# A two-layer encoder in fp32 parts: pairs that are split at once and pairs that stay whole take turns one by one in both MLPs

## The chip, the cores and the metric

The kernel runs on one core of a Trainium2 chip. Its engines are TensorE (PE: matrix products, with weight loads shown as PEld), VectorE (DVE), ScalarE (ACT), GpSimd (POOL) and SyncE (SP, which issues DMAs). Each works through its own queue in order, and semaphores between the queues carry the dependences. The metric is the device time of one execution in microseconds.

## The reference: what is computed

The input is 512 tokens of 1024 numbers. Layer 0 is a hybrid attention (grouped-query and latent heads), layer 1 a neighbourhood attention on an 8 x 64 grid, and behind each stands an MLP; a norm ends it. Only the MLPs matter here:

```
def sq_relu_mlp(h, w_up, w_down):
    u = jax.nn.relu(h @ w_up)
    return (u * u) @ w_down

h = h + sq_relu_mlp(rmsnorm(h, norm_ffn[layer]), ffn_w_up[layer], ffn_w_down[layer])
```

`w_up` is 1024 x 4096 and `w_down` 4096 x 1024, all in float32.

## The kernel before

**Numbers in two parts.** To keep float32 accuracy, every operand of a product is held as a high part (rounded to the matmul's format, `F32R`) and a low part (what the rounding left). Each product is three matmuls: high by high, high by low, low by high. So every weight chunk and every activation must be split: ScalarE copies the high part, VectorE subtracts it from the source to get the low part.

**Products with seven parts.** A part of the MLP's products is done by a scheme of the class `Seven`: a 2 x 2 arrangement of blocks is multiplied with seven block products in place of eight, at the price of sums of weights before (GpSimd, L357 to L359) and sums of results behind (VectorE, L459 to L462, after a copy of ScalarE at L458). A weight chunk of this kind is `seven_chunk`: SP loads 256 rows by 256 columns (L352) into a raw tile; GpSimd makes the sums; ScalarE makes the high part `whi` (L363, three buffers), VectorE the low part `wlo` (L364, four buffers). One call of `Seven.run`, a **pass** below, gives two result tiles of 128 x 512 (a **pair**): four chunks, each with 7 x 3 = 21 matmuls (L450 to L452), so 84 matmuls. Passes take turns between two groups of PSUM banks (named s, t, t, o and mm, mm, mm, s), so that the results of one are taken away during the next.

**The stages of one MLP.** `first_product` makes the tiles of the squared relu. Its first stage makes six of them, and a part of the second product follows. Its second stage, the long first product, has 13 passes, numbered 0 to 12 here, for the remaining 26 tiles. Then come `product8`, which uses eight of these tiles as plain split operands, a product by `Seven` over pairs that `convert` turns into its operands, and a rest. The first MLP's long first product runs from 322 to 451 us of the profile and the second's from 883 to 1013 us.

**Two kinds of pairs.** In a pass, the end `evac` receives the pair in one tile `w_` of 128 x 1024. For kind 0, **split at once** (`pair_evac`, L1400), the pair is one of the four whose eight tiles `product8` needs: two more tiles are taken for its parts. For kind 1, **whole** (`raw_evac`, L1395), `w_` is kept as it is for later stages. Either way `finish` (L1380) does the rest in three steps, which the loop in `stage` puts behind the 15th, 22nd and 25th of the 28 block products of the next pass: Relu (L1382) and Square (L1383) on ScalarE; for a split pair, then, for each of its two tiles a copy on ScalarE (L1388) and a subtraction on VectorE (L1389). These four kinds of instructions are held in the order of the program (`held`); most others are placed by the planner of the framework, which orders each engine's queue by its own cost model and by what is ready.

**Memory.** Tiles of 128 x 1024 come from 32 slots (`Slot`), given out in turn, the longest free first. The long first product's operand takes 14 of them. Each whole pair keeps one; the first two split pairs keep two each and give `w_` back, the third keeps one and the fourth none, since three of their tiles lie in spare buffers. Weight chunks load into a free slot if more than three are free, else into one of four raw buffers; they are asked for five chunks ahead (`LOAD`) and split two ahead (`AHEAD`).

The order of the kinds is a list in `stage`, L1450 and L1451, which is called with `n` = 8 tiles to be split and 16 or 14 that stay whole for the seven-part product, and 2 or 4 more for the rest. The list of split pairs' row numbers also gives `product8` the rows of `w_down`, and that of whole pairs gives them to the next product.

Of the kernel before, what the change touches and what calls it, by code (L numbers as in the profile page):

```python
# [35 lines left out]
def encoder_kernel(ctx: ExitStack, tc: tile.TileContext, ins, out, dbg=None):  # L36
# [1304 lines left out]
    def first_product(l):  # L1341
# [68 lines left out]
        def plain():  # L1410
            four = product(w, 0, xp, tiles(0, 512), ev, lambda n: [mmb(), mmb(), mmb(), sbk()])
            two = product(w, 0, xp, tiles(512, 256), ev, lambda n: [sbk(), ob()], kstep=4)
            for n, _ in enumerate(four):
                if n == (11 if l == 0 else 13):
                    norm()
                if n == 14:
                    x_sums(0)
                    x_sums(1)
            for n, _ in enumerate(two):
                if n == 4:  # L1420
                    x_sums(2)
                if n == 6:
                    x_sums(3)
            flip[0] = 1
            for s_ in X:
                s_.free()
            state["plain"] = True
# [9 lines left out]
        def ahead():  # L1437
            state["ids"] = x7.plan(w, P * state["c"])

        def stage(n, raw=0, more=0):  # L1440


            at = [], []
            if not state["plain"]:
                plain()
                at[0].extend(range(0, n, 2))
            nu, nr = (n - len(U)) // 2, raw // 2
            state["n"], state["halves"] = n, raw

            kinds = ([1, 0, 0] * ((nu + 1) // 2))[: nu + (nu + 1) // 2] if nr else [0] * nu  # L1450
            kinds += [1] * (nr + nu - len(kinds)) + [1] * (more // 2)  # L1451
            for i, kind in enumerate(kinds):
                ids = state["ids"]
                if i < nu + nr:
                    at[kind].append(state["c"])
                state["c"] += 2
                if i < len(kinds) - 1:
                    ahead()
                for u, _ in enumerate(x7.run(ids, (pair_evac, raw_evac)[kind])):
                    if u in (14, 21, 24):  # L1460
                        next(state["late"], None)
            if state["c"] == 32:
                x7.free()
            got = U[:n], R[: raw // 2], R[raw // 2 :], at, state["late"]
            U.clear()
            R.clear()
            return got

        return stage, ahead, later


# [603 lines left out]
```

## Time and profile before

| | us |
|---|---|
| median of three runs | 1163.75 (1161.8 to 1165.85) |
| the profiled execution | 1162.95 |
| its span, first to last instruction | 1161.2 |
| TensorE busy | 1146.3 |
| VectorE busy | 901.3 |
| ScalarE busy | 669.2 |
| GpSimd busy | 586.4 |

The rows of the profile name a line of the kernel, an engine, an operation and the tiles written and read (`out<-in`); groups have a count, the busy time, the mean of one in ns and the idle time of the engine before it, with what ended that. Rows in order of time begin with the start and the duration in us and end, where the engine was idle, with the idle time and its releaser in square brackets. A matmul's duration reaches to its modelled end, so successive matmuls overlap: their spacing is read from their starts.

### The profile page before, as it was taken

How to read it: one execution, taken by the hardware profiler on the slowest of the kernel's cores; microseconds unless marked ns; L12 is line 12 of the kernel's file. 1: busy time of each engine (PE TensorE's matmuls, PEld its weight loads, DVE VectorE, ACT ScalarE, POOL GpSimd, SP SyncE). 2: the span in 40 equal slices, each digit the busy share in tenths (PEclk: the TensorE clock that was granted, in tenths of full speed). 3: DMA queues.
4: the chain of work that ended last, by engine and by line, in shares of the span. 5: the costliest groups of instructions: out<-in, count | busy, mean ns of one | idle time of the engine just before them, and what ended most of it. 6: DMA issues, size and time to landing. Idle time of an engine off the chain costs nothing.

```text
span 1161.2 us, 20538 instructions
## 1 busy us (share of the span) xinstructions
PE 1146.3 (99%) x7348; PEld 1022.4 (88%) x7348; DVE 901.3 (78%) x1568; ACT 669.2 (58%) x1135; POOL 586.4 (51%) x719
## 2 busy tenths in 40 slices
PE   9999999999999999999999999999999999999997
PEld 7787888888899999899988998988889999989996
DVE  6887988878868876877785666668996787688865
ACT  6676877755346668543454556555543666774445
POOL 4356252207688992369502232231388799435840
PEclk9999999999999999999999999999999999999999
DMA  7322415222523327723536564433343233381432
GB/s 235 105 77 69 97 55 137 64 69 95 171 77 91 100 83 199 214 88 112 155 92 163 148 175 128 116 110 116 113 143 116 83 92 91 71 202 56 127 119 73
DMA packets 115350, 134.37 MB, mean 116 GB/s; under 512 B 9795, under 2 KB 96752, under 8 KB 115248
## 3 DMA queue, kind: packets, MB, share of 16 engines
q1 hardware_dynamic: 110896, 120.09, 34.9%
q0 software_dynamic: 4032, 12.60, 5.4%
q8 instruction: 58, 0.95, 0.3%
q10 hardware_dynamic: 320, 0.36, 0.1%
q14 instruction: 44, 0.36, 0.1%
HBM read 110.61 MB, written 6.29 MB: 101 GB/s over the span
## 4 chain that ended last, share of the span: by engine, by line
PE 87%; DVE 5%; DMA 2%; issue 2%; ACT 1%; POOL 1%; SPq 0%; DVEq 0%; ACTq 0%; POOLq 0%
PE mm L606 8%; PE mm L607 8%; PE mm L608 8%; PE mm L452 4%; PE mm L450 4%; PE mm L451 4%; PE s L1130 3%; PE o L1118 3%; PE t L450 3%; PE t L452 3%; PE t L451 3%; PE s L608 2%; PE s L606 2%; PE s L607 2%; PE t L1105 2%
## 5 line engine op out<-in xcount | busy, mean ns | idle before, releaser
L606 PE MATMUL mm<-a,whi 128*128 128x512 f32 x428 | 173.8, 407 | 0.2
L364 DVE TENSOR_TENSOR wlo<-a,whi 128x896 fp32r<-128x896 f32 x103 | 130.7, 1272 | 55.3 <-ACT whi L363 54.9
L607 PE MATMUL mm<-a,whi 128*128 128x512 f32 x428 | 169.0, 395 | 0.0
L608 PE MATMUL mm<-a,wlo 128*128 128x512 f32 x428 | 168.9, 396 | 0.0
L363 ACT ACTIVATE whi<-a 128x896 fp32r<-128x896 f32 x103 | 97.6, 948 | 105.0 <-PE o L607 27.6
L233 ACT ACTIVATE whi<-raw 128x1024 fp32r<-128x1024 f32 (+3 forms) x100 | 92.1, 924 | 68.5 <-PE s L607 24.3
L223 DVE TENSOR_TENSOR wlo<-raw,whi 128x1024 fp32r<-128x1024 f32 (+4 forms) x97 | 110.0, 1139 | 27.2 <-ACT whi L233 26.7
L452 PE MATMUL mm<-a,wlo 128*128 128x256 f32 x430 | 120.6, 280 | 0.3 <-DVE wlo L364 0.3
L450 PE MATMUL mm<-a,whi 128*128 128x256 f32 x430 | 120.7, 281 | 0.0
L451 PE MATMUL mm<-a,whi 128*128 128x256 f32 x430 | 120.3, 280 | 0.0
L363 ACT ACTIVATE whi<-raw 128x896 fp32r<-128x896 f32 x61 | 57.9, 952 | 80.5 <-POOL raw L359 37.9
L359 POOL TENSOR_TENSOR a<-a 128x128 f32<-128x128 f32 x103 | 99.3, 964 | 8.1
L364 DVE TENSOR_TENSOR wlo<-raw,whi 128x896 fp32r<-128x896 f32 x61 | 73.2, 1214 | 36.0 <-ACT whi L363 36.0
L358 POOL TENSOR_TENSOR a<-a 128x256 f32<-128x256 f32 x103 | 93.7, 910 | 8.1
L608 PEld LDWEIGHTS mm<-a,wlo 128*128 128x128 f32 x428 | 80.3, 188 | 18.2
L606 PEld LDWEIGHTS mm<-a,whi 128*128 128x128 f32 x428 | 80.5, 188 | 17.2 <-issue 0.8
L607 PEld LDWEIGHTS mm<-a,whi 128*128 128x128 f32 x428 | 80.7, 189 | 15.1 <-DVE a L655 0.3
L1718 POOL TENSOR_SCALAR p<-p,ti 128x256 f32<-128x256 f32 x64 | 36.0, 574 | 105.4 <-DVE ti L1717 90.4
L1138 POOL TENSOR_SCALAR p<-p,ti 128x512 f32<-128x512 f32 x64 | 45.5, 711 | 86.0 <-DVE ti L1137 61.4
L450 PE MATMUL t<-a,whi 128*128 128x256 f32 x312 | 87.7, 281 | 0.0
L452 PE MATMUL t<-a,wlo 128*128 128x256 f32 x312 | 87.3, 280 | 0.0
L451 PE MATMUL t<-a,whi 128*128 128x256 f32 x312 | 87.3, 280 | 0.0
(432 smaller groups left out, 3577.2 us busy)
## 6 DMA issues: line engine op xcount, KB each, us to landing
a<-in_ffn_w_up_dram SPq DMA_DIRECT2D x102, 256.0 KB, 2.8
raw<-in_ffn_w_down_dram SPq DMA_DIRECT2D x34, 512.0 KB, 4.1
raw<-in_ffn_w_down_dram SPq DMA_DIRECT2D x59, 256.0 KB, 2.6
raw<-in_od_w_qkv_dram SPq DMA_DIRECT2D x64, 128.0 KB, 3.0
raw<-in_ffn_w_up_dram SPq DMA_DIRECT2D x12, 512.0 KB, 3.9
wlo<-in_ffn_w_down_dram POOLq DMA_DIRECT2D x12, 512.0 KB, 6.7
a<-a SPq DMA_DIRECT2D x18, 256.0 KB, 3.3
bx<-a SPq DMA_DIRECT2D x32, 128.0 KB, 6.0
```

Of the source, the lines that this page charges most:

```text
L223: z = lambda: (eng or DVE).tensor_tensor(to, src, f32(high), op=ALU.subtract)
L233: ACT.activation(hi[:, 0:m], raw[:, 0:m], AF.Copy)
L358: held(eng.tensor_tensor(r[:, 4:6], r[:, 2:3].to_broadcast([P, 2, P]), r[:, 0:7:6], op=ALU.add))
L359: held(eng.tensor_tensor(r[:, 7], r[:, 3], r[:, 5], op=ALU.subtract))
L363: ACT.activation(hi[:, 0:896], raw[:, 128:1024], AF.Copy)
L364: DVE.tensor_tensor(lo[:, 0:896], raw[:, 128:1024], f32(hi[:, 0:896]), op=ALU.subtract)
L450: PE.matmul(o, wh, x[:, 0], start=kp == 0 and n in (0, 1, 3, 5), stop=False, skip_group_check=True)
L451: PE.matmul(o, wh, x[:, 1], start=False, stop=False, skip_group_check=True)
L452: PE.matmul(o, wl, x[:, 0], start=False, stop=kp == self.np - 1, skip_group_check=True)
L606: PE.matmul(o, wh, xh, start=first, stop=False)
L607: PE.matmul(o, wh, xl, start=False, stop=False)
L608: PE.matmul(o, wl, xh, start=False, stop=last)
```

## The change

In the list of kinds, where there are whole pairs at all, whole and split pairs now alternate one by one until all four split pairs are placed; before, two split pairs followed each whole one. What follows the fourth split pair is whole in both.

```diff
-            kinds = ([1, 0, 0] * ((nu + 1) // 2))[: nu + (nu + 1) // 2] if nr else [0] * nu
+            kinds = [1, 0] * nu if nr else [0] * nu
             kinds += [1] * (nr + nu - len(kinds)) + [1] * (more // 2)
```

With four split pairs the 13 passes become (0 is split at once, 1 is whole), in both MLPs:

```
pass      0 1 2 3 4 5 6 7 8 9 10 11 12
before    1 0 0 1 0 0 1 1 1 1 1  1  1
after     1 0 1 0 1 0 1 0 1 1 1  1  1
```

## The prediction

> **What bounds the kernel now.** I read the page first, then the waits of TensorE, then the order of time on TensorE, ScalarE and VectorE in the stretch that the change touches.
>
> ```profile
> span 1161.2 us, 20538 instructions
> ...
> PE 1146.3 (99%) x7348; PEld 1022.4 (88%) x7348; DVE 901.3 (78%) x1568; ACT 669.2 (58%) x1135; POOL 586.4 (51%) x719
> ...
> L364 DVE TENSOR_TENSOR wlo<-a,whi 128x896 fp32r<-128x896 f32 x103 | 130.7, 1272 | 55.3 <-ACT whi L363 54.9
> ```
>
> TensorE is busy for 99% of the span, so a change that takes no matrix product away can win only what TensorE loses in waits. The third row is VectorE's making of a weight chunk's low part, 1.27 us each; without it the third matmul of each triple cannot go. The view of who waited for whom, for TensorE (total, times, longest):
>
> ```profile
> PE s L452 <- DVE wlo L364: 2.0, 3, 1.1
> ...
> PE s L608 <- DVE wlo L223: 0.5, 1, 0.5
> ...
> PE mm L452 <- DVE wlo L364: 0.3, 1, 0.3
> ```
>
> Nearly all that TensorE waits for in the MLPs is that low part. To see where, TensorE in order of time: the first matmul of pass 0 and of pass 12 of each MLP's long first product, the first one behind pass 12, then pass 6, pass 7, and the two long waits.
>
> ```profile
> 322.21 0.28 PE L450 MATMUL mm<-a,whi 128*128 128x256 f32 x1
> ...
> 381.56 0.28 PE L450 MATMUL mm<-a,whi 128*128 128x256 f32 x1
> ...
> 391.45 0.28 PE L450 MATMUL s<-a,whi 128*128 128x256 f32 x1
> ...
> 396.52 0.28 PE L451 MATMUL s<-a,whi 128*128 128x256 f32 x1
> 397.17 0.38 PE L452 MATMUL s<-a,wlo 128*128 128x256 f32 x1 [0.38 <-DVE wlo L364]
> ...
> 441.54 0.28 PE L450 MATMUL mm<-a,whi 128*128 128x256 f32 x1
> ...
> 882.63 0.28 PE L450 MATMUL mm<-a,whi 128*128 128x256 f32 x1
> ...
> 957.47 0.28 PE L451 MATMUL s<-a,whi 128*128 128x256 f32 x1
> 958.87 0.38 PE L452 MATMUL s<-a,wlo 128*128 128x256 f32 x1 [1.13 <-DVE wlo L364]
> ...
> 1003.11 0.28 PE L450 MATMUL mm<-a,whi 128*128 128x256 f32 x1
> ...
> 1012.98 0.44 PE L606 MATMUL s<-a,whi 128*128 128x512 f32 x1
> ```
>
> The last two rows give an undisturbed pass: 1012.98 - 1003.11 = 9.87 us for 84 matmuls, 0.12 us apart. Twelve passes should take 118.44 us. They took 441.54 - 322.21 = 119.33 us in the first MLP and 1003.11 - 882.63 = 120.48 us in the second: 0.89 and 2.04 us too long. In both, the longest wait lies in pass 7, at the third chunk: the matmul due 0.12 us behind the one at 396.52 starts at 397.17 (0.53 us late), the one behind 957.47 starts 1.28 us late.
>
> **Why just there.** Passes 0 to 6 carry the kinds whole, split, split, whole, split, split, whole. The finishing work of a pair is done during the pass behind it and over that pass's end. ScalarE's Relu of each pair, in passes 3 to 7:
>
> ```profile
> 358.74 1.06 ACT L1382 ACTIVATE a<-a 128x1024 f32<-128x1024 f32 x1 [0.83 <-DVE a L462]
> ...
> 369.75 1.06 ACT L1382 ACTIVATE a<-a 128x1024 f32<-128x1024 f32 x1 [1.94 <-DVE a L462]
> ...
> 377.71 1.06 ACT L1382 ACTIVATE a<-a 128x1024 f32<-128x1024 f32 x1
> ...
> 388.53 1.06 ACT L1382 ACTIVATE a<-a 128x1024 f32<-128x1024 f32 x1 [0.94 <-DVE a L462]
> ...
> 399.35 1.06 ACT L1382 ACTIVATE a<-a 128x1024 f32<-128x1024 f32 x1 [1.87 <-DVE a L462]
> ```
>
> With passes 9.87 us apart from 322.21, passes 3, 4 and 5 begin near 351.8, 361.7 and 371.6, so the Relu comes 6.9, 8.1 and 6.1 us into them; in passes 6 and 7 (381.56, 391.45) 7.0 and 7.9 us in. It is latest in passes 4 and 7, behind the second split pair of each two, and ScalarE, waiting for the last addition L462, holds back the high part of the next chunk. VectorE at the starts of pass 6 and pass 7:
>
> ```profile
> 380.74 1.25 DVE L364 TENSOR_TENSOR wlo<-a,whi 128x896 fp32r<-128x896 f32 x1 [0.85 <-ACT whi L363]
> 381.91 0.95 DVE L1389 TENSOR_TENSOR a<-a,a 128x512 fp32r<-128x512 f32 x1
> 382.78 0.95 DVE L1389 TENSOR_TENSOR bias<-a,bias 128x512 fp32r<-128x512 f32 x1
> 383.65 0.68 DVE L459 TENSOR_TENSOR a<-a,t 128x512 f32<-128x512 f32 x1
> 384.24 1.08 DVE L364 TENSOR_TENSOR wlo<-a,whi 128x896 fp32r<-128x896 f32 x1
> ...
> 391.56 1.31 DVE L364 TENSOR_TENSOR wlo<-a,whi 128x896 fp32r<-128x896 f32 x1 [2.03 <-ACT whi L363]
> 392.79 0.95 DVE L1389 TENSOR_TENSOR p<-a,p 128x512 fp32r<-128x512 f32 x1
> 393.66 0.67 DVE L459 TENSOR_TENSOR a<-a,mm 128x512 f32<-128x512 f32 x1
> 394.25 1.17 DVE L1389 TENSOR_TENSOR p<-a,p 128x512 fp32r<-128x512 f32 x1
> 395.35 0.68 DVE L460 TENSOR_TENSOR a<-a,mm 128x512 f32<-128x512 f32 x1
> 395.95 1.17 DVE L364 TENSOR_TENSOR wlo<-a,whi 128x896 fp32r<-128x896 f32 x1
> ```
>
> Both hold the two subtractions of a split pair (L1389). Pass 6 finishes the first of two: its first low part starts 0.82 us ahead of the pass and the third chunk's ends at 385.32, 3.8 us into it. TensorE needs that 5.2 us in (half a pass and two matmuls): 1.4 us to spare. Pass 7 finishes the second: it starts 0.93 us later against its pass, with the addition L460 put ahead of the low part, which ends at 397.12, 5.7 us in. That is the wait. The lateness comes from two L1389 in the pass before, by way of L462, Relu and the high part.
>
> **The change, part by part.** (1) Split pairs go from passes 1, 2, 4, 5 to 1, 3, 5, 7 in both MLPs. Nothing is added: the same matmuls, chunks, Relus and 8 splits, in another order. (2) Each split pair now follows a whole one, so its two subtractions find VectorE as pass 6 did. Behind them comes a pass without any, like pass 5, whose Relu waited for nothing: the lateness no longer adds up. Expected gain: 0.53 to 0.89 us in the first MLP, I take 0.7, the middle; and 2.0 us in the second, where nearly all the excess lies in passes 3 to 7. Sum 2.7 us. Bound from below: with pass 7's worse order but the start 0.93 us earlier, the first MLP has no wait (0.53 - 0.93 is under zero) and the second still 1.28 - 0.93 = 0.35 us; at all four split pairs that is 1.4 us, leaving 1.3. (3) The last split pair ends two passes later, in passes 8 and 9. Its reader, the eight-tile second product, starts behind pass 12, three passes or 30 us on: no cost. (4) Slots: a split pair holds up to three while it is split, a whole one keeps one. Counting them by the code, passes 4, 6, 7 and 8 have one slot fewer free than now, passes 3 and 5 two and one more; passes 9 to 12 stand as now. SP's weight loads go into these slots, so a few can start up to one chunk (9.87 / 4 = 2.5 us) later, and with them GpSimd's sums. The nearest rows, a chunk's last sum on GpSimd and its first reader on ScalarE, at pass 8's first chunk:
>
> ```profile
> 386.96 1.19 POOL L359 TENSOR_TENSOR a<-a 128x128 f32<-128x128 f32 x1
> ...
> 396.53 0.95 ACT L363 ACTIVATE whi<-a 128x896 fp32r<-128x896 f32 x1 [1.52 <-PE o L451]
> ...
> L359 POOL TENSOR_TENSOR a<-a x103: 461/1190/1337, 287.5 to 1056.9; 128x128 f32<-128x128 f32 x103
> ```
>
> The sum ends at 388.15 and is read 8.4 us later, when TensorE frees a buffer; 2.5 us are covered, cost zero. (5) The second products read other rows in another order: as many loads of the same size on the same queues, taken as zero, between -1.3 and +1.3 us, the sum of the waits left (third rival). No added instruction waits; behind the moved L1389 VectorE queues the four additions and the low parts, already counted.
>
> Sum: 1162.95 us, the profiled execution (0.8 us below the median 1163.75), minus 2.7 is 1160.25; against the median 1161.05. I say 1161.0.
>
> One rule bears on this. The last quoted row has the same subtraction on GpSimd take 0.46 us at least, 1.19 us at the median: something holds it for 0.73 us. The Trainium skill, "SBUF — State Buffer", section "Who interferes with whom", says that a VectorE instruction with two SBUF inputs and a GpSimd instruction that reads SBUF exclude each other for the whole instruction. L1389 has two such inputs, so by that rule the change moves GpSimd delays to passes with fewer free slots. The spread of that row agrees with it, and VectorE's rows of 0.95 and 1.17 us for one L1389 too. What it would make of the sum is the last rival.
>
> **Rivals.**
> *More goes than the stretch itself (faster).* The waits view leaves 2.0 - 0.38 - 1.13 = 0.49, 0.33 and 0.53 us in the second products. A wait costs more than its idle time (0.38 us idle was 0.53 to 0.89 lost), so some 2 us in all. Everything behind is placed anew by the planner, and these are near misses. For it: each is under 0.55 us. Against: their chunks are not of the product changed. All gone: 1163.75 - 2.7 - 2.0 = 1159.0.
> *Each split pair stalls (slower).* Place: VectorE's queue at the start of passes 3, 5, 7 and 9. If the planner puts L460 and both L1389 ahead of the third low part each time, and passes between do not recover, each of the four costs what pass 7 does now: 0.7 and 1.4 us, 4 x 2.1 = 8.4 for both MLPs, minus 2.7 of now: +5.7, 1169.5. It decides where the third low part ends over 5.2 us into its pass. Against: pass 6 ended at 3.8, and pass 5 shows a Relu without wait in one pass.
> *Nothing happens.* New waits of some 0.7 us replace the old: 1163.5. For it: the second MLP lost time in passes 4 and 5 too.
> *GpSimd becomes late (slower).* At its worst: each L1389 blocks GpSimd once, 4 pairs x 2 x 0.73 = 5.8 us in each MLP, all before pass 8; with 2.5 us of later loads 8.3 us, just inside the cover of 8.4 us, so nothing. Blocked twice for each, it is 11.7 + 2.5 - 8.4 = 5.8 us uncovered in each MLP: 1163.75 - 2.7 + 11.6 = 1172.7. Against: most L359 rows are slow already, with L1389 or without. This is the rule of the Trainium skill's "SBUF — State Buffer", section "Who interferes with whom", taken to its end; without it the sum stays 1161.0.
>
> **How the numbers follow.** 0.3% is 3.5 us, about what a measurement of this kernel can tell from no change. Forecast 0.40 (its own range 1160.8 to 1162.5, from gains of 2.9 and 1.3 us, within the bound); nothing happens 0.08: within 0.3% is 0.48. More goes 0.30: faster. Stalls at each pair 0.19, GpSimd late 0.03: slower 0.22. The range runs from 1157.5 (1.5 us of scatter below 1159.0) to 1169.0, almost the whole of the slower case; outside lie half of that case and a little of the faster one.
>
> **What would show it.** Right: the first matmuls of passes 0 and 12 are 118.4 to 118.9 us apart in both MLPs; no wait of TensorE on L364 there; Relus 6 and 7 us into their passes in turn, none at 8. Wrong: TensorE rows with a wait for L364 in passes 3, 5, 7 or 9, Relu still at 8 us, ScalarE's L363 waiting for GpSimd's L359 in passes 6 to 8, or lost time in stretches that the change does not touch.

## The result and the profile after

The changed kernel takes 1160.4 us at the median against 1163.86 us for the kernel before: the ratio is 0.9972, with a 95% interval of 0.9965 to 0.9979, so 2.4 to 4.1 us faster and 3.3 us in the middle. The forecast was 2.7 us. Measured again in a later session the ratio was 0.9969 (0.9959 to 0.9979).

The page of the profile after:

```profile
span 1158.0 us, 20534 instructions
...
PE 1145.2 (99%) x7348; PEld 1022.7 (88%) x7348; DVE 893.7 (77%) x1568; ACT 669.2 (58%) x1135; POOL 585.3 (51%) x719
...
L364 DVE TENSOR_TENSOR wlo<-a,whi 128x896 fp32r<-128x896 f32 x103 | 125.4, 1219 | 59.1 <-ACT whi L363 58.6
```

Each engine's count of instructions is the same, and the span is 3.2 us shorter. TensorE's waits after the change (total, times, longest):

```profile
PE s L452 <- DVE wlo L364: 1.2, 1, 1.2
...
PE mm L452 <- DVE wlo L364: 0.4, 1, 0.4
```

Of the three waits of the first row before, one is left, and it is in the second product. The wait on L223 is gone too. TensorE in order of time, at the first matmul of pass 0, of pass 12 and of the next product, in both MLPs:

```profile
321.88 0.28 PE L450 MATMUL mm<-a,whi 128*128 128x256 f32 x1
...
440.59 0.28 PE L450 MATMUL mm<-a,whi 128*128 128x256 f32 x1
...
450.48 0.40 PE L606 MATMUL s<-a,whi 128*128 128x512 f32 x1
...
882.27 0.28 PE L450 MATMUL mm<-a,whi 128*128 128x256 f32 x1
...
1000.91 0.28 PE L450 MATMUL mm<-a,whi 128*128 128x256 f32 x1
...
1010.80 0.39 PE L606 MATMUL s<-a,whi 128*128 128x512 f32 x1
```

Passes 0 to 11 now take 440.59 - 321.88 = 118.71 us and 1000.91 - 882.27 = 118.64 us, against 119.33 and 120.48 us: 0.62 and 1.84 us less. The Relus of passes 3 to 7 show why:

```profile
358.40 1.07 ACT L1382 ACTIVATE a<-a 128x1024 f32<-128x1024 f32 x1 [0.82 <-DVE a L462]
...
367.38 1.04 ACT L1382 ACTIVATE a<-a 128x1024 f32<-128x1024 f32 x1
...
377.76 1.06 ACT L1382 ACTIVATE a<-a 128x1024 f32<-128x1024 f32 x1 [0.39 <-DVE a L462]
...
387.16 1.05 ACT L1382 ACTIVATE a<-a 128x1024 f32<-128x1024 f32 x1
...
397.88 1.06 ACT L1382 ACTIVATE a<-a 128x1024 f32<-128x1024 f32 x1 [0.72 <-DVE a L462]
```

With passes 9.89 us apart from 321.88, they come 6.9, 5.9, 6.4, 5.9 and 6.8 us into their passes: late and on time by turns, and none at 8 us. VectorE at the start of pass 7, which now finishes a split pair behind a whole one:

```profile
390.18 1.16 DVE L364 TENSOR_TENSOR wlo<-a,whi 128x896 fp32r<-128x896 f32 x1 [1.34 <-ACT whi L363]
391.26 0.95 DVE L1389 TENSOR_TENSOR a<-a,a 128x512 fp32r<-128x512 f32 x1
392.13 0.95 DVE L1389 TENSOR_TENSOR bias<-a,bias 128x512 fp32r<-128x512 f32 x1
393.00 0.67 DVE L459 TENSOR_TENSOR a<-a,mm 128x512 f32<-128x512 f32 x1
393.60 1.08 DVE L364 TENSOR_TENSOR wlo<-a,whi 128x896 fp32r<-128x896 f32 x1
```

It is the picture of pass 6 before: the first low part starts 0.9 us ahead of the pass (391.1), the third chunk's ends at 394.68, 3.6 us into it. Over passes 3, 5, 7 and 9 of both MLPs it ends 3.2 to 4.2 us in, where TensorE needs it 5.2 us in, so there are 1.0 to 2.0 us to spare.

**Where the 3.2 us of the span came from**, stretch by stretch, each from the first matmul of a product to the first of the next, before and after, in us:

| stretch | before | after |
|---|---|---|
| first MLP, long first product | 129.23 | 128.60 |
| first MLP, eight-tile second product | 44.14 | 44.05 |
| first MLP, seven-part second product | 80.70 | 81.29 |
| second MLP, long first product | 130.35 | 128.53 |
| second MLP, eight-tile second product | 44.88 | 43.99 |

The two long products give 2.45 us. Another 0.89 us is the wait on L223 that is gone, and 0.59 us is lost at the longer wait of the first MLP's seven-part second product. The remaining 0.4 us or so lies outside these rows, 0.33 us of it ahead of the first long product, which the change doesn't touch. Only the long products repeat: a second profile of the change, shown at the end of the experiments, has the same two lengths but a span of 1160.1 us, 2.1 us above the first.

### The profile page after: what moved, and what is told of

It reads as the page before. It is cut to its first block, busy times and chain, and to the rows that moved or that the text cites. A ratio compares the mean times of both kernels' runs of the same rounds, so it can differ in the third digit from the quotient of the medians.

```text
span 1158.0 us, 20534 instructions
## 1 busy us (share of the span) xinstructions
PE 1145.2 (99%) x7348; PEld 1022.7 (88%) x7348; DVE 893.7 (77%) x1568; ACT 669.2 (58%) x1135; POOL 585.3 (51%) x719
## 4 chain that ended last, share of the span: by engine, by line
PE 89%; DVE 5%; DMA 3%; ACT 1%; issue 1%; POOL 0%; SPq 0%; DVEq 0%; POOLq 0%; ACTq 0%
PE mm L606 8%; PE mm L607 8%; PE mm L608 8%; PE mm L452 4%; PE mm L450 4%; PE mm L451 4%; PE s L1130 3%; PE t L450 3%; PE t L452 3%; PE t L451 3%; PE o L1118 3%; PE s L452 2%; PE s L450 2%; PE s L451 2%; PE t L1105 2%; PE s L606 2%
## 5 line engine op out<-in xcount | busy, mean ns | idle before, releaser
L364 DVE TENSOR_TENSOR wlo<-a,whi 128x896 fp32r<-128x896 f32 x103 | 125.4, 1219 | 59.1 <-ACT whi L363 58.6
L233 ACT ACTIVATE whi<-raw 128x1024 fp32r<-128x1024 f32 (+3 forms) x100 | 92.2, 924 | 68.4 <-PE s L607 24.3
L223 DVE TENSOR_TENSOR wlo<-raw,whi 128x1024 fp32r<-128x1024 f32 (+4 forms) x97 | 110.4, 1143 | 26.9 <-ACT whi L233 26.4
L358 POOL TENSOR_TENSOR a<-a 128x256 f32<-128x256 f32 x103 | 97.8, 950 | 8.1
L364 DVE TENSOR_TENSOR wlo<-raw,whi 128x896 fp32r<-128x896 f32 x61 | 73.6, 1221 | 35.0 <-ACT whi L363 35.0
L359 POOL TENSOR_TENSOR a<-a 128x128 f32<-128x128 f32 x103 | 95.7, 929 | 8.1
```

Of the source, the lines that this page charges most:

```text
L223: z = lambda: (eng or DVE).tensor_tensor(to, src, f32(high), op=ALU.subtract)
L233: ACT.activation(hi[:, 0:m], raw[:, 0:m], AF.Copy)
L358: held(eng.tensor_tensor(r[:, 4:6], r[:, 2:3].to_broadcast([P, 2, P]), r[:, 0:7:6], op=ALU.add))
L359: held(eng.tensor_tensor(r[:, 7], r[:, 3], r[:, 5], op=ALU.subtract))
L364: DVE.tensor_tensor(lo[:, 0:896], raw[:, 128:1024], f32(hi[:, 0:896]), op=ALU.subtract)
```

## The experiments

**Theory and rivals.** The theory is the prediction's: two split pairs in a row make VectorE, then ScalarE's Relu, then the next high and low parts late, and one whole pair between them clears that. The rivals are that the number of split pairs matters and not their order, that ScalarE's copies or the slots make the lateness, and that the rows which the second products read change the time.

**One MLP at a time.** In the first experiment the list depends on the layer.

```diff
-            kinds = [1, 0] * nu if nr else [0] * nu
+            kinds = ([1, 0] * nu if l else [1, 0, 0] * 2) if nr else [0] * nu
```

> The new order in the second MLP only. Theory (lateness adds up over two split pairs in a row, and the gain of the first MLP is given back at the first chunk wait of its seven-part second product): passes 0 to 12 of the second MLP take 118.4 to 118.7 us instead of 120.5, its 0.53 us wait on L223 is gone as well, the first MLP stays as before; time about 2.9 us below before, 1161.0, ratio 0.9975. Rival (both MLPs share the gain in the proportion of their lost time, 0.9 to 2.0): 2.2 us, ratio 0.9981.

Measured: 0.998 (0.9972 to 0.9989), 1161.62 us. The second MLP's long product took 128.26 us and its eight-tile product 44.11 us, about as short as with the change. The interval holds both expectations, 0.9975 and 0.9981. The first MLP, with the order of before, took 129.60 us here against 129.23: a stretch with waits does not repeat as one without them does. The other way round, with the new order in the first MLP alone:

```diff
-            kinds = [1, 0] * nu if nr else [0] * nu
+            kinds = ([1, 0, 0] * 2 if l else [1, 0] * nu) if nr else [0] * nu
```

> The new order in the first MLP only. Theory: its passes 0 to 12 win 0.6 to 0.9 us, and the wait on L364 at the third chunk of its second product grows by as much, since that chunk's loads land when they did: no gain, 1163.8 plus or minus 0.5, ratio 1.000. Rival (the gain is kept): 0.7 to 1.0 us faster, ratio 0.9992.

Measured: 0.9996 (0.9986 to 1.0006), 1163.06 us. The long product took 128.60 us, 0.63 less than before, but the interval holds both expectations. The second MLP gives most of the gain; whether the first MLP's 0.6 us reaches the end can't be told from the times. The wait in the first pass of its seven-part product was 1.09 us long here, against 0.48 us in the profile before. (A pass of that product has eight chunks of 21 matmuls. The wait is at the pass's 24th matmul, so at the second chunk; the expectations call it the third.) It was also 1.09 us in the run ahead of this one, whose first MLP is that of before, with its vector, scalar and GpSimd instructions in the same order:

```profile
500.45 0.38 PE L452 MATMUL s<-a,wlo 128*128 128x256 f32 x1 [1.09 <-DVE wlo L364]
```

So that wait does not grow because TensorE comes earlier. It differs between executions of the same order of instructions, and the "given back" of my expectation is not shown.

**Four in a row.**

```diff
-            kinds = [1, 0] * nu if nr else [0] * nu
+            kinds = [1] + [0] * nu if nr else [0] * nu
```

> Four split pairs in a row (passes 1 to 4). Theory: the lateness of the second is passed on, so waits on L364 come in passes 4, 5 and 6 of both MLPs, three of them with some 0.7 us in the first and 1.4 us in the second: 6.3 us lost against 2.9 before, so about 3 us slower than before, 1167, ratio 1.003. Rival (the number of split pairs sets the loss, not their order, and the change's gain is from elsewhere): within 1 us of before.

Measured: 1.0018 (1.0009 to 1.0027), 1166.41 us. Order alone makes the kernel slower than before, so the number of split pairs is not what counts. Its Relus of passes 3 to 6:

```profile
359.09 1.06 ACT L1382 ACTIVATE a<-a 128x1024 f32<-128x1024 f32 x1 [0.65 <-DVE a L462]
...
370.08 1.06 ACT L1382 ACTIVATE a<-a 128x1024 f32<-128x1024 f32 x1 [1.75 <-DVE a L462]
...
380.68 1.07 ACT L1382 ACTIVATE a<-a 128x1024 f32<-128x1024 f32 x1 [2.45 <-DVE a L462]
...
391.29 1.06 ACT L1382 ACTIVATE a<-a 128x1024 f32<-128x1024 f32 x1 [2.50 <-DVE a L462]
```

ScalarE's wait for VectorE's last addition grows over the first three, 0.65, 1.75, 2.45 us, and hardly any more at the fourth, 2.50 us, by when TensorE is itself late. TensorE paid in the first MLP here:

```profile
377.96 0.39 PE L452 MATMUL s<-a,wlo 128*128 128x256 f32 x1 [0.42 <-DVE wlo L364]
...
389.11 0.38 PE L452 MATMUL mm<-a,wlo 128*128 128x256 f32 x1 [1.01 <-DVE wlo L364]
```

These are the third chunks of passes 5 and 6, and the second MLP has waits at the same two (0.50 and 1.56 us). Pass 4 had no wait: I had three of them and there were two.

**The suspected cost taken away.** This run keeps the order of before and cuts both subtractions of a split pair to 16 columns. The rest of these low parts is set to zero by GpSimd.

```diff
-                    held(DVE.tensor_tensor(d[:, 1, :], src, f32(d[:, 0, :]), op=ALU.subtract))
+                    held(DVE.tensor_tensor(d[:, 1, 0:16], src[:, 0:16], f32(d[:, 0, 0:16]), op=ALU.subtract))
...
                 U.append(to[-1])
+                POOL.memset(f32(to[-1].pair()[:, 1, 16:S]), 0.0)
```

> The order of before, with the two subtractions of a split pair (L1389) cut to 16 of 512 columns; the rest of the low part is set to zero by GpSimd, so this computes the eight split tiles without most of their low parts. Theory (L1389 at the start of a pass makes the lateness): no wait on L364 in passes 0 to 12 of either MLP, their lengths 128.6 and 128.5 us from the first matmul to the next product, although two split pairs still stand in a row; time about 1160.5, ratio 0.997. Rival (ScalarE's copies L1388 or the slots that split pairs hold make it): the waits of pass 7 stay, 1163.9.

Measured: 0.9987 (0.9978 to 0.9995), 1162.54 us. The long products took 128.60 and 128.33 us, as expected to 0.2 us, with the copies and the slots as before: it is the subtractions, and neither of these two rivals. The total was less than expected, since both waits behind stayed, among them

```profile
1012.88 0.50 PE L608 MATMUL s<-a,wlo 128*128 128x512 f32 x1 [0.53 <-DVE wlo L223]
```

So the wait on L223 does not come from the late passes.

**How much room is left.** In the changed order, one subtraction more for each pair, then two more.

```diff
                     held(DVE.tensor_tensor(d[:, 1, :], src, f32(d[:, 0, :]), op=ALU.subtract))
+                    if z:
+                        held(DVE.tensor_tensor(d[:, 1, :], src, f32(d[:, 0, :]), op=ALU.subtract))
```

> The changed order, with the second tile's subtraction L1389 done twice: three a pair in place of two. Theory (1.4 us to spare behind a split pair, 0.95 us for one L1389): the third low part still comes in time, no wait in passes 0 to 12, time as with the change, 1160.4, ratio 0.997. Rival (no room is left): waits of 0.5 us or more at each of the four split pairs, 1163 or more.

Measured: 0.9997 (0.9988 to 1.0006), 1163.34 us. The expectation fell: with three, waits came back in both MLPs, the longest of each being

```profile
416.83 0.39 PE L452 MATMUL s<-a,wlo 128*128 128x256 f32 x1 [0.40 <-DVE wlo L364]
...
977.51 0.39 PE L452 MATMUL s<-a,wlo 128*128 128x256 f32 x1 [0.25 <-DVE wlo L364]
```

and the long products took 129.44 and 129.23 us. These two are the third chunks of pass 9. VectorE's queue there, first with the change, then in this run (L1391 is the added subtraction):

```profile
413.29 0.68 DVE L460 TENSOR_TENSOR a<-a,mm 128x512 f32<-128x512 f32 x1
413.89 1.18 DVE L364 TENSOR_TENSOR wlo<-a,whi 128x896 fp32r<-128x896 f32 x1
415.00 0.41 DVE L461 TENSOR_TENSOR a<-a,mm 128x256 f32<-128x256 f32 x1
...
414.45 0.78 DVE L1391 TENSOR_TENSOR p<-a,p 128x512 fp32r<-128x512 f32 x1
415.15 0.41 DVE L461 TENSOR_TENSOR a<-a,mm 128x256 f32<-128x256 f32 x1
415.48 1.30 DVE L364 TENSOR_TENSOR wlo<-a,whi 128x896 fp32r<-128x896 f32 x1
```

With the change the low part ends 4.2 us into the pass (415.07, the pass starts at 410.91), although L460 is ahead of it as in pass 7 before: the earlier start is enough. Here it ends 5.7 us in (416.78, from 411.09), since the addition L461 now goes ahead of it too. So the room was not overrated, the price of a subtraction was: one more made the third low part of passes 3, 5, 7 and 9 0.9 to 1.7 us later, and passes 3, 7 and 9 lost up to 0.7 us each.

```diff
                     held(DVE.tensor_tensor(d[:, 1, :], src, f32(d[:, 0, :]), op=ALU.subtract))
+                    held(DVE.tensor_tensor(d[:, 1, :], src, f32(d[:, 0, :]), op=ALU.subtract))
```

> The changed order, with both subtractions L1389 done twice: four a pair. Theory: 1.9 us more at the start of the pass is 0.5 us above what was to spare, so a wait on L364 at the third chunk in passes 3, 5, 7 and 9 of both MLPs, 0.5 to 1.0 us lost each: 4 to 8 us in all against the change, 1164 to 1168. Rival (VectorE's room over a whole pass counts, not its queue at the start): it still has room in the pass without L1389, so no wait, 1160.4.

Measured: 1.0094 (1.008 to 1.0108), 1175.01 us, 14.6 us above the change's median, nearly twice the most that was expected. The waits came where expected, in passes 3, 5, 7 and 9 of both MLPs, but at 1.0 to 1.7 us each, so the rival is out. VectorE at the start of pass 3 shows what else happened (L1390 is the added subtraction):

```profile
352.29 0.95 DVE L1389 TENSOR_TENSOR a<-a,a 128x512 fp32r<-128x512 f32 x1
353.15 0.68 DVE L459 TENSOR_TENSOR a<-a,mm 128x512 f32<-128x512 f32 x1
353.75 1.17 DVE L1390 TENSOR_TENSOR a<-a,a 128x512 fp32r<-128x512 f32 x1
354.84 0.95 DVE L1389 TENSOR_TENSOR a<-a,a 128x512 fp32r<-128x512 f32 x1
355.71 0.68 DVE L460 TENSOR_TENSOR a<-a,mm 128x512 f32<-128x512 f32 x1
356.31 0.68 DVE L1390 TENSOR_TENSOR a<-a,a 128x512 fp32r<-128x512 f32 x1
356.91 0.41 DVE L461 TENSOR_TENSOR a<-a,mm 128x256 f32<-128x256 f32 x1
357.24 1.08 DVE L364 TENSOR_TENSOR wlo<-a,whi 128x896 fp32r<-128x896 f32 x1
```

and TensorE's wait for that low part:

```profile
358.38 0.39 PE L452 MATMUL s<-a,wlo 128*128 128x256 f32 x1 [1.26 <-DVE wlo L364]
```

The planner let two more additions, L460 and L461, go ahead of the low part. More work in that queue costs its own time and that of the work that slips ahead.

**Farther apart.**

```diff
-            kinds = [1, 0] * nu if nr else [0] * nu
+            kinds = ([1, 0, 1] * nu)[:-1] if nr else [0] * nu
```

> Two whole pairs between split pairs (split in passes 1, 4, 7, 10). Theory: one pass without split subtractions is enough to clear the lateness, so nothing more is won: no wait in passes 0 to 12, time as with the change, 1160.4 plus or minus 0.7, ratio 0.997. Rival (the farther apart the better, since some lateness is left after one pass): another 1 us or more.

Measured: 1.0 (0.9991 to 1.0009), 1163.9 us; both expectations are wrong. Inside the long products it is as expected: no wait, and 128.60 us in the first MLP. The gain is lost behind them. In the second MLP, TensorE waits 0.76 us for a high part (L233) at the first matmul behind pass 12. More goes in the first pass of the first MLP's seven-part product; the whole product took 84.30 us in place of 81.29:

```profile
497.09 0.39 PE L450 MATMUL t<-a,whi 128*128 128x256 f32 x1 [0.56 <-DVE hT L1538]
...
498.76 0.38 PE L450 MATMUL o<-a,whi 128*128 128x256 f32 x1 [0.69 <-DVE hT L1538]
...
501.56 0.38 PE L452 MATMUL s<-a,wlo 128*128 128x256 f32 x1 [1.40 <-DVE wlo L364]
```

There VectorE was late with the conversion of the whole pairs and stood 2.0 us before a sum of weights, L357, until that chunk's load had landed (0.9 us after the change). Whether the order of the kinds moved that load is not settled.

**The rows alone.** The order of before, with each pair given the columns that it has after the change:

```diff
+            wholes, splits = [6, 10, 14, 18, 22, 24, 26, 28, 30], [8, 12, 16, 20]
+            order = [wholes.pop(0) if z else splits.pop(0) for z in kinds] + [32]
...
-                state["c"] += 2
+                state["c"] = order[i + 1]
```

> The order of before (two split pairs behind each whole one), but each pair takes the columns that it has after the change, so that the second products read the same rows of weights in the same order as after the change. Theory: the rows cost nothing, so all is as before: the waits in pass 7 of both MLPs stay, and the wait of 0.5 us on L223 behind the second MLP's pass 12 too; 1163.9, ratio 1.000. Rival (the rows set the wait on L223): that wait goes, 0.8 us faster, ratio 0.9993.

Measured: 0.9994 (0.9982 to 1.0007), 1163.11 us. The waits of pass 7 stayed:

```profile
396.71 0.39 PE L452 MATMUL s<-a,wlo 128*128 128x256 f32 x1 [0.21 <-DVE wlo L364]
...
959.10 0.38 PE L452 MATMUL s<-a,wlo 128*128 128x256 f32 x1 [0.55 <-DVE wlo L364]
```

The long products took 129.07 and 129.60 us, 0.2 and 0.8 us less than before. Differences of that size come without any change of rows: the MLPs that keep the order of before took 129.60 and 131.01 us in the two runs that change one MLP only. The rows do not make the change's gain: its interval ends at 0.9979, and this one begins at 0.9982. But the wait on L223 was not there. It was there in each of the other four runs that kept the second MLP's order of before or put the split pairs together (before, first MLP alone, four in a row, short subtractions), while with the new order there it was gone, but for 0.2 us lost in the two runs with added subtractions. That speaks for the rival, but one profile each can't tell whether the rows remove it or whether it comes and goes, and the interval of the time holds both expectations. It stays open.

**Can the wait behind be removed?** Three runs tried the wait at the second chunk of the first MLP's seven-part product, on top of the change. First, the fourth chunk's sums on GpSimd:

```diff
-            return [plan(w, pairs[kp] if pairs else 2 * kp, c0, DVE if pairs and kp == 3 else None, make=seven_chunk)
+            return [plan(w, pairs[kp] if pairs else 2 * kp, c0, None, make=seven_chunk)
```

> The changed kernel, with the sums L357 to L359 of the fourth chunk of each pass of the seven-part second products on GpSimd, as those of the other three chunks, and not on VectorE. Theory (in the first MLP VectorE stands 0.3 to 2.0 us before L357 until that chunk's load has landed, and the low part for which TensorE waits is behind it in VectorE's queue): the wait of 1.2 us at the third chunk of the first pass of that product goes, 1.5 us or more is won, 1158.9, ratio 0.996. Rival (GpSimd's sums then come late): TensorE waits for the fourth chunk's low part, no gain or a loss of 1 us or more.

Measured: 0.9982 (0.9973 to 0.999), 1161.84 us. The wait was 0.74 us long, but waits of 1.05 us came in the third and the fourth pass, both at the fourth chunk, as the rival has it. Then the same in the first pass only, with the condition `DVE if pairs and kp == 3 and c0 else None`:

> The changed kernel, with the fourth chunk's sums on GpSimd in the first pass of the seven-part second products only, and on VectorE in the other three. Theory: the wait at the third chunk of that first pass shrinks as with all four on GpSimd (to some 0.9 us lost in place of 1.4), and the two new waits of 1.2 us in the third and fourth pass do not come: 0.5 to 1.0 us faster than the change, 1159.6, ratio 0.9965. Rival (that wait is set by the rest of VectorE's queue): the same as the change, 1160.4, ratio 0.997.

Measured: 0.998 (0.9969 to 0.9991), 1162.03 us, with a wait of 1.40 us. That is the rival, but loosely shown: in the runs so far that leave these sums alone the same wait was 0.48 to 1.40 us long, so 0.74 and 1.40 us say little about the sums. Last, the two splits that stand right ahead of the low part moved two passes on:

```diff
-                if m == 0 and i % 8 == 4 and left:
+                if m == 2 and i % 8 == 4 and left:
```

> The changed kernel, with the first MLP's splitting of its last whole pair (two L963 on VectorE, 1.28 us together) moved from the first pass of the seven-part second product to the third. Theory (the wait at the third chunk of the first pass is VectorE's queue, in which the two L963 stand right ahead of that low part): the wait shrinks by about 1.2 us and no new one comes: 1 us faster than the change in the same session, ratio to before 0.9963. Rival (the low part would have been kept back by something else, ScalarE's high part or a load): the wait stays, the time is that of the change.

Measured: 0.9974 (0.9964 to 0.9984), 1160.66 us. The wait at that chunk is gone, as in none of the other profiles, so it was VectorE's queue; but another stands in the pass that took the splits:

```profile
543.74 0.38 PE L452 MATMUL s<-a,wlo 128*128 128x256 f32 x1 [0.79 <-DVE wlo L364]
```

In the same session the changed kernel itself ran once more.

> The changed kernel once more, in the same session as the run before: 1160.4, ratio 0.997. Its passes 0 to 12 take the same 128.6 and 128.5 us in a second profiled execution, if their length does not hang on the execution; the wait at the third chunk of the first MLP's seven-part second product, which was 0.6 to 1.6 us long in the runs so far, may differ from the first profile's 1.4 us by several tenths.

Measured: 0.9969 (0.9959 to 0.9979), 1161.31 us. Its long products took 128.60 and 128.53 us, to the hundredth what the first profile has. The waits behind did not repeat: 1.39 us in place of 1.22 at the second chunk, 0.86 in place of 0.36 us in the next pass, and a new one of 0.42 us for a load in the first MLP's eight-tile product. No version tried beats the change.

## Why the prediction was right, point by point

- **What bounds.** Right: TensorE was busy for 99% of both spans, and the gain is time that it no longer waits for low parts.
- **The lateness over two split pairs.** Right. Four in a row made it grow and cost some 2 us more than before; cutting the subtractions removed it without touching the order.
- **The size.** The long products gave 0.62 and 1.84 us in passes 0 to 11 where I had 0.7 and 2.0. In the first MLP an undisturbed pass is 9.89 us, not the 9.87 us that I took from one pass of the second, so 0.24 us of the 0.89 us were no excess. In the second MLP 9.87 us was right before, and passes 4, 5 and 7 gave back all their excess (10.04, 10.42 and 11.25 us became 9.88, 9.89 and 9.88); but every pass there takes 9.88 or 9.89 us after the change, in both its executions, which costs some 0.25 us. No run shows why.
- **The total.** 2.7 us was forecast and 3.3 us measured, and that they are so near is in part luck. The long products gave 2.45 us; the rest is what came and went behind them, 0.89 us won and 0.59 us lost, and scatter. The lost time in the seven-part product is one of the signs that I had named for being wrong. It doesn't count against the theory, since that wait was as long with the first MLP of before.
- **1.4 us to spare.** About right: 1.0 to 2.0 us with the change. What I had wrong, in the expectation of the run with three subtractions, was the price of one more: beside its own 0.7 to 1.2 us it lets an addition go ahead of the low part.
- **The last split pair's later end, the slots, GpSimd.** Right as far as TensorE goes: none of its waits in the changed passes is left, and GpSimd was busy for 585.3 us against 586.4. The profile does put some of ScalarE's idle time in passes 6 to 8 down to GpSimd's sums, up to 1.51 us at a time before and after, and I had named that as a sign of being wrong. But when sums and high parts are counted off in order, a chunk's last sum ended 7.5 us or more ahead of its high part in passes 3 to 9 before and 8.3 us or more after, so ScalarE did not wait for that, and no matmul was delayed after the change. The delays of GpSimd that I expected by the rule of the Trainium skill's "SBUF — State Buffer", section "Who interferes with whom", reached no matmul there; no run here isolates the rule.
- **Rows at zero.** Not told apart from zero: the rows alone gave 0.9994, 0.7 us in the middle and within the 1.3 us that I allowed, but the interval reaches to 2.1 us. The wait on L223 is the one that may hang on them.
- **More goes than the stretch itself.** A part of this rival came: of the three waits behind, the one on L223 went and won 0.89 us; the other two stayed, one of them longer by 0.74 us. Near misses moved both ways, so counting only removals was wrong.
- **Stalls at each split pair.** Did not come with the change; with twice the subtractions they came in the four passes that this rival named.

## What to carry to other kernels

When one engine bounds a kernel, look for the queue that feeds it and see whether extra jobs in that queue meet in consecutive periods: the total can fit and still be late, because each period hands its delay on to the next. Spreading the jobs so that one light period follows each heavy one was enough here; a wider spacing won nothing more, and in its one profile the gain was lost in the stages behind. What an added or moved job costs in a queue that a planner orders can't be read from its duration alone, since other work may slip ahead of the critical one.

## What the hardware showed that I had not expected

VectorE's low parts L364 are not of one length. In the same form they took 1.08 us and 1.54 us within a few rows of each other (pass 7 after the change), and the mean over 103 of them was 1272 ns before, 1219 ns after the change and 1242 ns in its second execution; 53 ns less each is 5.5 us of VectorE's time in a kernel whose instructions are the same:

```profile
393.60 1.08 DVE L364 TENSOR_TENSOR wlo<-a,whi 128x896 fp32r<-128x896 f32 x1
...
395.65 1.54 DVE L364 TENSOR_TENSOR wlo<-a,whi 128x896 fp32r<-128x896 f32 x1
397.11 0.68 DVE L462 TENSOR_TENSOR a<-a,s 128x512 f32<-128x512 f32 x1
397.71 1.17 DVE L364 TENSOR_TENSOR wlo<-a,whi 128x896 fp32r<-128x896 f32 x1
```

The long product's length did not change by that (128.60 us in both executions of the change), but a wait that is a near miss did: 1.22 and 1.39 us at the same chunk of the same kernel, and 0.48 and 1.09 us in two executions whose first MLP is that of before. The longer ones go with GpSimd's work: over all 14 profiles, the 274 low parts that lay beside no GpSimd instruction took 1.08 to 1.10 us each, and all 1555 that took more than 1.10 us lay beside one. The Trainium skill, "SBUF — State Buffer", section "Who interferes with whom", would put this down to VectorE's two SBUF inputs meeting GpSimd's reads. The rows agree with that, and nothing here was run to show it.
